# A place of their own for the weights of odd pairs, the first pair's sums on VectorE, the gelu's stores on SP's queue

## The chip, the cores and the metric

The kernel runs on one core of a Trainium2 chip. The metric is the device time of one execution, in microseconds (us); lower is better. The core has TensorE (PE, matrix multiply; PEld is its weight load), VectorE (DVE), ScalarE (ACT), GpSimd (POOL) and SyncE (SP). SP, ACT and POOL each have a queue on which transfers (DMAs) are issued; a queue works off its instructions in order, so an instruction that waits holds up all behind it.

## The reference

One decoder layer on 1024 tokens of width 1024, in float32:

```python
proj = x @ w_in                                   # one wide input projection, split into nine parts
y_a = rglru_branch(lru_x, lru_gate, ...)          # recurrent branch: h * gelu(lru_gate)
y_b = banded_window_attention(qb, kb, vb, 128, sinks)
y_c = dilated_attention(qc, kc, vc)               # three window/dilation patterns, combined
branch = einsum('bsnc,ncd->bsnd', stack([y_a, y_b, y_c]), w_branch)
merged = sum(sigmoid(gates) * branch, axis=2)     # gates: 3 x 1024 columns of proj
x = layer_norm(ALPHA * x + merged @ w_out)
h1, h3 = split(x @ w_ffn_in)                      # 2 x 2816 columns
x = layer_norm(ALPHA * x + (silu(h1) * h3) @ w_ffn_out)
```

What the change touches is the part of `x @ w_in` that makes the gates and the gelu gate, and `x @ w_ffn_in`.

## The kernel before

Every float32 matrix is split in two parts, a rounded one (hi, made by ScalarE with a copy to a 32-bit format that TensorE takes fast) and the rest (lo, made by VectorE with a subtraction). A product of 128x128 weights with 512 columns takes three matmuls: hi by hi, hi by lo, lo by hi.

The work runs in stages. First come the input projections, the recurrent branch and the two attentions (up to about 935 us). Then the **gate stage**: 12 pairs of gate columns and 3 pairs of gelu columns. Then the branch projections (`w_branch`), the output projection (`w_out`) with the first layer norm, the **FFN pairs** (22 of them), and `w_ffn_out` with the second layer norm.

A *pair* is two blocks of 128 weight columns, c = 0 and 1. The class `Pairs` (lines 832 to 987) computes both for all 1024 tokens with seven products in place of eight (a Strassen form of the 2x2 block product), each of 12 matmuls. The products are named by the operand of x: a00, s2, s1, s3, a01, s4, a11. For weights they need the blocks of the pair themselves (b0, b11) and four sums: t1, t2, t3 and t4. In a *fronted* pair a00 and a01 have been done in a stage before and their result is kept, so it has five products (60 matmuls); other pairs have seven (84). All 12 gate pairs and the first 4 FFN pairs are fronted; the gelu pairs (numbers 3, 6 and 9 of the gate stage's 15) and the other 18 FFN pairs aren't.

For each pair the weights go through this chain:
- `load` (line 878): two transfers of 512 KB on SP's queue, into two tiles with the tag w_raw. The pool `stage` has two such tiles in all, and both stages use it.
- `p1` (line 909): t1 and then t2 on POOL, each 128x512 (`wsum`, line 885). The tag t has two tiles.
- `wsplit` (line 890) of t2, then of t1: a copy on ScalarE into a tile ph, a subtraction on VectorE into a tile pl. There are 5 tiles of each in the gate stage (`n_p` = 5) and 7 in the FFN.
- `p5` (line 917): t3 on POOL, and its split. `p6` (line 921): t4 on POOL, written over t2 once that is split, then the split of b11 straight from the raw tile, then that of t4.
- `p2`, for a pair that isn't fronted: the split of the whole first raw tile, for a00 and a01.

`run` (line 971) strings them together. While pair j is computed, the steps for pair j+1 are issued at the seven points `between(i)` in front of j's products: `load` of j+1 at i = 1, `p1` and `p2` at 3, the split of t2 at 5, that of t1 and `p5` at 6, and `p6` of j+1 at its own i = 0. `p6` is the last to read the two raw tiles, so `load` of the next pair can't begin before it.

A product's result is added on VectorE (lines 946 to 968). A gate pair's four results are stored to sg_dram on ACT's queue. A gelu pair's four results go through `lg_finish` (line 692), two ScalarE and three VectorE instructions each, and its store to y_dram is issued on POOL's queue (line 699).

The operands s2, s3, s4 and part of the others are made by `x_sums` and `x_split` (lines 801, 1024) from four quarters of x; the last of these, number 3, lies in a tile of the pool `yx` (tag v, line 1032), and VectorE works on it when pair 0 begins. Later the same tile takes a quarter of the operand y for the branch stage (`load_y`, line 1060, called at pair 11). The transfers of `load_y` are issued on ACT's queue and carry an order-only dependence (line 1074) on the last copy of a weight that `wsplit` made.

The order of the instructions on each engine isn't written by hand alone: the program is given to a planner, which orders each engine's instructions by priority and by times that it simulates (`schedule_with_timeline_sim=True`). The chip then runs each engine in that order.

Of the kernel before, what the change touches and what calls it, by code (L numbers as in the profile page):

```python
# [9 lines left out]
F32 = mybir.dt.float32  # L10
# [33 lines left out]
class WeightStream:  # L44
# [41 lines left out]
    def _split(self):  # L86
        c = self.n_split
        self._dma(c + 2)
        raw = self.raw.pop(c)
        if self.dests[c] is None:  # L90
            hi = self.pool.tile([P, 1024], F32R, tag="w_hi", name="w_hi")
            lo = self.pool.tile([P, 1024], F32R, tag="w_lo", name="w_lo")
            self.ring.append(c)
        else:
            hi, lo = self.dests[c]()
        self.nc.scalar.copy(hi, raw)  # L96
        self.lo_engine.tensor_sub(lo, raw, hi.bitcast(F32))  # L97
        self.parts[c] = (hi, lo)
        self.n_split += 1
        self._dma(c + 3)  # L100
# [48 lines left out]
def trunk_kernel(ctx: ExitStack, tc: tile.TileContext, x, x_t, w_in, conv_w, conv_b, w_rg, b_rg, w_ig, b_ig,  # L149
# [542 lines left out]
    def lg_finish(ct, hf, z, u, hh):  # L692

        act.activation(u, z, AF.Square, scale=math.sqrt(0.044715))
        dve.scalar_tensor_tensor(u, u, 1.0, z, op0=OP.add, op1=OP.mult)
        act.activation(u, u, AF.Tanh, scale=math.sqrt(2.0 / math.pi))
        dve.scalar_tensor_tensor(u, u, 1.0, z, op0=OP.add, op1=OP.mult)
        dve.scalar_tensor_tensor(u, u, 0.5, hh, op0=OP.mult, op1=OP.mult)
        pool.dma_start(y_dram[0][ct, :, hf * HALF:(hf + 1) * HALF], u)
# [4 lines left out]
    def lg_evac(ct):  # L704
        def f(hf, acc):
            u, hh = [att4.tile([P, HALF], F32, tag=n, bufs=1, name=n) for n in ("gelu", "hh")]
            load_h(ct, hf, hh)
            lg_finish(ct, hf, acc, u, hh)
        return f
# [120 lines left out]
    recent = []  # L830

    class Pairs:
# [3 lines left out]
        def __init__(self, cols, ops, ring, p1pool, fronted, na, c00, c01, c10, c11, n_e=6, n_p=7):  # L836
            self.fronted = fronted
            self.cols, self.ops, self.ring, self.p1pool, self.na = cols, ops, ring, p1pool, na
            self.c00, self.c01, self.c10, self.c11 = c00, c01, c10, c11
            self.n_e, self.n_p = n_e, n_p  # L840
            self.raws, self.parts, self.front = {}, {}, {}
# [36 lines left out]
        def load(self, j):  # L878
            self.raws[j] = []
            for c in self.cols(j):  # L880
                t = stage.tile([P, 1024], F32, tag="w_raw", name="w_raw")
# [3 lines left out]
        def wsum(self, j, n, a, b, op):  # L885
            t = self.ring[0].tile([P, HALF], F32, tag="t", bufs=2, name="t")
            pool.tensor_tensor(t, a, b, op=op)  # L887
            self.raws[j, n] = t

        def wsplit(self, j, n, src, width=HALF):  # L890
            if width == HALF:
                hi = self.ring[0].tile([P, HALF], F32R, tag="ph", bufs=self.n_p, name="ph")
                lo = self.ring[0].tile([P, HALF], F32R, tag="pl", bufs=self.n_p, name="pl")
# [3 lines left out]
            recent[:] = [act.copy(hi, src)]  # L897
# [73 lines left out]
        def run(self, n, at=lambda j, i: None, first=None, done=0):  # L971

            first = first or self.prep(0)
            for f in first[done:6]:
                f()
            for j in range(n):
# [3 lines left out]
                def between(i):  # L980
                    if i == 0:
                        cur[6]()
                    elif nxt:
                        for f in {1: nxt[:1], 3: nxt[1:3], 5: nxt[3:4], 6: nxt[4:6]}.get(i, ()):
                            f()
                    at(j, i)
# [21 lines left out]
    def pair_out(j, c, hf, src):  # L1008
# [7 lines left out]
        else:  # L1016
            u, hh = [t[:, 2 * hf + c, :] for t in lgt]
            lg_finish(kinds[j] + c, hf, src, u, hh)

    gate = Pairs(pair_cols, xops, [gring], [gring], lambda j: j in gid, NG,  # L1020
                 lambda j, bank: pair_out(j, 0, 0, bank), lambda j, g: pair_out(j, 1, 0, g),
                 lambda j, g: pair_out(j, 0, 1, g), lambda j, v: pair_out(j, 1, 1, v), 4, 5)
# [37 lines left out]
    def load_y(n, hf):  # L1060
# [11 lines left out]
        for k in range(KT):  # L1072
            d = act.dma_start(yl[k].bitcast(F32), y_dram[n][k, :, hf * HALF:(hf + 1) * HALF])
            tc.add_manual_dep(d.ins, recent[-1].ins.name, NO_SYNC, reason="not earlier than the pairs' weights")
# [322 lines left out]
    ffn = Pairs(lambda j: [w_cols(w_ffn_in, c) for c in (j * P, FF + j * P)], ops, sringp, [frp], lambda j: j < NA, NA,  # L1397
# [152 lines left out]
```

## Time and profile before

| | us |
|---|---|
| median of 3 runs | 2243.51 (2243.04 to 2245.42) |
| the profiled execution, its own time | 2241.2 |
| its span, first to last instruction | 2239.4 |
| TensorE busy | 2170.8 (97%) |
| VectorE busy | 1424.7 (64%) |
| ScalarE busy | 969.7 (43%) |
| POOL busy | 559.5 (25%) |
| mean granted TensorE clock | 0.992 of full speed |

"Busy" is the time in which an engine had an instruction under way; matmuls are pipelined, so a new one begins each 0.23 us though each lasts 0.39 us. In a row of the timeline, what stands in square brackets is the idle time of the engine in front of that instruction and what ended it. The rows themselves stand in a section below.

### The profile page before, as it was taken

How to read it: one execution, taken by the hardware profiler on the slowest of the kernel's cores; microseconds unless marked ns; L12 is line 12 of the kernel's file. 1: busy time of each engine (PE TensorE's matmuls, PEld its weight loads, DVE VectorE, ACT ScalarE, POOL GpSimd, SP SyncE). 2: the span in 40 equal slices, each digit the busy share in tenths (PEclk: the TensorE clock that was granted, in tenths of full speed). 3: DMA queues.
4: the chain of work that ended last, by engine and by line, in shares of the span. 5: the costliest groups of instructions: out<-in, count | busy, mean ns of one | idle time of the engine just before them, and what ended most of it. 6: DMA issues, size and time to landing. Idle time of an engine off the chain costs nothing. (4 is left out here: it accounts for less than half of the span.)

```text
span 2239.4 us, 29667 instructions
## 1 busy us (share of the span) xinstructions
PE 2170.8 (97%) x10981; PEld 1834.5 (82%) x10981; DVE 1424.7 (64%) x2695; ACT 969.7 (43%) x1826; POOL 559.5 (25%) x506
## 2 busy tenths in 40 slices
PE   8999999999999999899999999999999999999998
PEld 6787888988889888677777888888788888888786
DVE  7888888876777776655565334459565444453735
ACT  4765766665655656522324223223333333332321
POOL 2332222212222234233341000002344444300301
PEclk9999999999999999999999999999999999999999
DMA  5123123122222144444457334244232222254543
GB/s 151 48 80 97 48 65 81 49 48 64 48 56 56 30 105 139 130 137 137 141 174 253 131 106 132 94 146 154 87 104 85 85 85 85 85 193 148 183 157 119
DMA packets 228401, 241.57 MB, mean 108 GB/s; under 512 B 11489, under 2 KB 170273, under 8 KB 228257
## 3 DMA queue, kind: packets, MB, share of 16 engines
q1 hardware_dynamic: 184864, 135.28, 19.9%
q0 software_dynamic: 18336, 57.73, 8.8%
q10 hardware_dynamic: 25056, 46.67, 6.1%
q8 instruction: 86, 1.41, 0.3%
q14 instruction: 59, 0.48, 0.1%
HBM read 177.51 MB, written 51.64 MB: 102 GB/s over the span
## 5 line engine op out<-in xcount | busy, mean ns | idle before, releaser
L187 PE MATMUL acc<-xh,w_hi 128*128 128x512 f32 x688 | 274.6, 399 | 13.0 <-ACT w_hi L96 6.9
L187 PE MATMUL acc<-xl,w_hi 128*128 128x512 f32 x688 | 272.1, 395 | 0.0
L187 PE MATMUL acc<-xh,w_lo 128*128 128x512 f32 x688 | 271.6, 395 | 0.0
L96 ACT CAST w_hi<-w_raw 128x1024 fp32r<-128x1024 f32 x130 | 136.7, 1052 | 242.9 <-PE acc L187 192.5
L897 ACT CAST ph<-t 128x512 fp32r<-128x512 f32 x148 | 89.7, 620 | 309.6 <-POOL t L887 219.7
L887 POOL TENSOR_TENSOR t<-w_raw 128x512 f32<-128x512 f32 x74 | 109.0, 1472 | 313.8 <-DMA w_raw<-in_w_ffn_in_dram 193.8
L97 DVE TENSOR_TENSOR w_lo<-w_raw,w_hi 128x1024 fp32r<-128x1024 f32 x89 | 113.8, 1279 | 112.2 <-ACT w_hi L96 111.9
L898 DVE TENSOR_TENSOR pl<-t,ph 128x512 fp32r<-128x512 f32 x148 | 111.3, 759 | 113.0 <-ACT ph L897 112.9
L187 PEld LDWEIGHTS acc<-xh,w_hi 128*128 128x128 f32 x688 | 130.4, 189 | 38.8 <-ACT w_hi L96 6.9
L539 POOL DMA_DIRECT2D y_dram<-yp x96 | 51.6, 537 | 428.4 <-DVE yp L538 341.0
L549 DVE TENSOR_TENSOR pt_l<-pt,pt_h 128x512 fp32r<-128x512 f32 (+3 forms) x256 | 144.2, 572 | 21.3 <-ACT pt_h L548 19.0
L548 ACT CAST pt_h<-pt 128x512 fp32r<-128x512 f32 (+3 forms) x256 | 124.4, 501 | 70.1 <-PE pt L544 65.5
L187 PEld LDWEIGHTS acc<-xh,w_lo 128*128 128x128 f32 x688 | 130.1, 189 | 25.5 <-DVE w_lo L97 0.8
L187 PEld LDWEIGHTS acc<-xl,w_hi 128*128 128x128 f32 x688 | 130.4, 190 | 23.5
L544 PE MATMUL pt<-ident,p 128*128 128x128 f32 x816 | 128.0, 276 | 4.3 <-DVE pt_l L549 3.5
L97 POOL TENSOR_TENSOR w_lo<-w_raw,w_hi 128x1024 fp32r<-128x1024 f32 x41 | 98.9, 2412 | 113.0 <-ACT w_hi L96 106.9
L187 PE MATMUL o<-pt_h,v 128*128 128x256 f32 (+1 forms) x464 | 117.0, 274 | 2.0 <-DVE yp L538 1.5
L187 PE MATMUL acc<-w_lo,gh 128*128 128x512 f32 x288 | 113.5, 394 | 4.1 <-DVE w_lo L97 4.0
L631 ACT ACTIVATE p<-p,small 128x128 f32<-128x128 f32 (+7 forms) x128 | 99.7, 779 | 34.9 <-DVE small L628 33.8
L187 PE MATMUL o<-pt_l,v 128*128 128x256 f32 (+1 forms) x464 | 113.1, 284 | 1.3 <-DVE pt_l L549 1.3
L187 PE MATMUL acc<-w_hi,gl 128*128 128x512 f32 x288 | 112.8, 392 | 0.0
L187 PE MATMUL s<-kh,q 128*128 128x256 f32 (+3 forms) x320 | 104.4, 335 | 1.7 <-DVE small L628 1.0
(303 smaller groups left out, 5927.6 us busy)
## 6 DMA issues: line engine op xcount, KB each, us to landing
w_raw<-in_w_in_dram SPq DMA_DIRECT2D x88, 512.0 KB, 3.9
w_raw<-in_w_ffn_in_dram SPq DMA_DIRECT2D x48, 512.0 KB, 3.8
w_raw<-in_w_ffn_out_dram SPq DMA_DIRECT2D x47, 512.0 KB, 3.7
w_raw<-in_w_branch_dram SPq DMA_DIRECT2D x24, 512.0 KB, 4.9
sg<-sg_dram POOLq DMA_DIRECT2D x24, 512.0 KB, 3.9
g_dram<-e POOLq DMA_DIRECT2D x44, 256.0 KB, 3.2
sg_dram<-e ACTq DMA_DIRECT2D x39, 256.0 KB, 2.6
yl<-y_dram ACTq DMA_DIRECT2D x32, 256.0 KB, 6.0
```

What stands on the lines that cost most here:

```text
L96: self.nc.scalar.copy(hi, raw)
L97: self.lo_engine.tensor_sub(lo, raw, hi.bitcast(F32))
L187: pe.matmul(o, a, b, start=start, stop=stop, skip_group_check=True)
L539: pool.dma_start(dst, yp[:, :n])
L544: pe.transpose(pt[:, i * P:(i + 1) * P], b, ident)
L548: act.copy(dst_h, v)
L549: dve.tensor_sub(dst_l, v, dst_h.bitcast(F32))
L631: act.activation(p[:, :n], p[:, :n], AF.Exp, bias=m, scale=-1.0, accum_out=sm[:, 1:2])
L887: pool.tensor_tensor(t, a, b, op=op)
L897: recent[:] = [act.copy(hi, src)]
L898: dve.tensor_sub(lo, src, hi.bitcast(F32))
```

## The change

1. **Place.** `load` no longer takes its tiles from the tag w_raw alone but from a function `room`. Even pairs use w_raw as before. Odd pairs of the gate stage use the tile v of `yx` (pairs 1 to 9) and then the two tiles with the tag w_hi (pairs 11 and 13). Odd pairs of the FFN use two tiles of their own in the FFN's ring; in exchange the ring has 5 tiles ph and pl of each where it had 7.
2. **Order of issue.** `load(1)` is issued ahead of the first pair, and `load(j+2)` at `between(1)` of pair j. `p1` of j+1 moves from point 3 to 1, `p2` and the split of t2 to 2, the split of t1 to 3, `p5` to 4.
3. **First sums.** t1, t2 and t3 of pair 0 of the gate stage are computed on VectorE, not on POOL. (t4 stays on POOL.)
4. **Stores.** The four stores of a gelu pair are issued on SP's queue, the one that also loads the weights, not on POOL's.
5. **Order of y.** The order-only dependence of `load_y` is now on the last weight copy of any kind, also on those of the stream `W` that feeds the branch stage.

```diff
 class WeightStream:
-        self.nc.scalar.copy(hi, raw)
+        self.recent = self.nc.scalar.copy(hi, raw)
 ...
-    def lg_finish(ct, hf, z, u, hh):
+    def lg_finish(ct, hf, z, u, hh, queue):
-        pool.dma_start(y_dram[0][ct, :, hf * HALF:(hf + 1) * HALF], u)
+        queue.dma_start(y_dram[0][ct, :, hf * HALF:(hf + 1) * HALF], u)
 ...
         def load(self, j):
             self.raws[j] = []
-            for c in self.cols(j):
-                t = stage.tile([P, 1024], F32, tag="w_raw", name="w_raw")
+            for i, c in enumerate(self.cols(j)):
+                t = self.room(j, i)
                 sync.dma_start(t.rearrange("p (a b) -> p a b", b=P), c)
 ...
         def wsum(self, j, n, a, b, op):
-            pool.tensor_tensor(t, a, b, op=op)
+            (dve if self is gate and j == 0 else pool).tensor_tensor(t, a, b, op=op)
 ...
-                hi = self.ring[0].tile([P, HALF], F32R, tag="ph", bufs=self.n_p, name="ph")
-                lo = self.ring[0].tile([P, HALF], F32R, tag="pl", bufs=self.n_p, name="pl")
+                hi = self.ring[0].tile([P, HALF], F32R, tag="ph", bufs=5, name="ph")
+                lo = self.ring[0].tile([P, HALF], F32R, tag="pl", bufs=5, name="pl")
 ...
-            recent[:] = [act.copy(hi, src)]
+            W.recent = act.copy(hi, src)
 ...
+            self.load(1)
             for j in range(n):
 ...
-                        for f in {1: nxt[:1], 3: nxt[1:3], 5: nxt[3:4], 6: nxt[4:6]}.get(i, ()):
+                        for f in {1: nxt[1:2], 2: nxt[2:4], 3: nxt[4:5], 4: nxt[5:6]}.get(i, ()):
                             f()
+                        if i == 1 and j + 2 < n:
+                            self.load(j + 2)
 ...
+    def gate_room(j, i):
+        if j % 2 == 0:
+            return raw_tile()
+        if j > NP - 2:
+            return raw_tile("w_hi")
+        if not spare:
+            spare.append(yx.tile([P, 4, HALF], F32, tag="v", name="w_raw"))
+        return spare[0].rearrange("p a b -> p (a b)")[:, i * D:(i + 1) * D]
 ...
-            tc.add_manual_dep(d.ins, recent[-1].ins.name, NO_SYNC, reason="not earlier than the pairs' weights")
+            tc.add_manual_dep(d.ins, W.recent.ins.name, NO_SYNC, reason="not earlier than the pairs' weights")
 ...
     ffn = Pairs(...,
+                lambda j, i: raw_tile() if j % 2 == 0 else sringp[0].tile([P, 1024], F32, tag="w_raw", bufs=2, name="w_raw"),
```

## Rows read from the trace of the kernel before

**Rows 1.** Busy time by stretch. Columns: stretch and its length in us; busy us and number of instructions of PE, PEld, DVE, ACT, POOL; granted TensorE clock; share of the DMA engines; GB/s. The gate stage, and the part of the FFN pairs that aren't fronted.

```profile
945.00:1185.00 240.00, 223.97 (x945) 181.64 (x944) 137.19 (x201) 70.21 (x120) 90.06 (x72) 0.96 0.46 145
1650.00:1935.00 285.00, 284.83 (x1257) 235.59 (x1256) 142.39 (x201) 89.83 (x139) 119.16 (x93) 1.00 0.27 86
```

**Rows 2.** Who PE waited for, 930 to 1220 us: us in total, times, longest. Then the same for 1570 to 2010 us.

```profile
PE acc L187 <- ACT ph L897: 15.8, 6, 4.7
...
PE acc L187 <- ACT ph L897: 4.2, 3, 1.6
```

**Rows 3.** PE's timeline in the gate stage: start, us, what, and the idle time in front. First the first and the last of 48 matmuls without a gap, then the five instructions in front of which PE had waited more than 1 us for a weight.

```profile
965.81 0.39 PE L187 MATMUL acc<-gs2h,ph 128*128 128x512 f32 x1
976.46 0.39 PE L187 MATMUL acc<-gs4h,pl 128*128 128x512 f32 x1
...
949.90 0.50 PE L187 MATMUL acc<-gs2h,ph 128*128 128x512 f32 x1 [3.19 <-ACT ph L897]
978.10 0.50 PE L187 MATMUL acc<-gs2h,ph 128*128 128x512 f32 x1 [1.25 <-ACT ph L897]
1026.87 0.80 PE L187 MATMUL acc<-gs2h,ph 128*128 128x512 f32 x1 [4.71 <-ACT ph L897]
1079.15 0.50 PE L187 MATMUL acc<-gs2h,ph 128*128 128x512 f32 x1 [2.98 <-ACT ph L897]
1130.40 0.50 PE L187 MATMUL acc<-gs2h,ph 128*128 128x512 f32 x1 [3.02 <-ACT ph L897]
```

**Rows 4.** Busy time by stretch (columns as in rows 1): the four stretches of 20 us in the gate stage in which the granted clock is below 1.00, and the one in which the branch stage begins.

```profile
945.00:965.00 20.00, 16.61 (x65) 12.80 (x64) 12.60 (x17) 6.59 (x13) 10.04 (x6) 0.91 0.36 113
1025.00:1045.00 20.00, 18.13 (x68) 14.77 (x69) 9.80 (x14) 5.09 (x8) 7.48 (x8) 0.83 0.40 132
1065.00:1085.00 20.00, 17.02 (x68) 13.45 (x67) 13.97 (x22) 7.04 (x12) 7.22 (x8) 0.91 0.51 169
1125.00:1145.00 20.00, 16.98 (x68) 13.43 (x67) 10.58 (x16) 4.04 (x7) 9.98 (x8) 0.91 0.56 174
1205.00:1225.00 20.00, 18.88 (x83) 14.98 (x82) 14.27 (x21) 14.78 (x22) 1.06 (x2) 1.00 0.77 271
```

**Rows 5.** Who the queue of SP waited for, and who POOL waited for, 945 to 1185 us.

```profile
SPq L882 <- POOL t L923: 136.3, 14, 12.3
...
POOL y_dram L699 <- DVE u L698: 20.7, 6, 4.9
```

**Rows 6.** The chain of work that ended last, where it passes through the weights of one gate pair: start, us, what.

```profile
1156.21 3.67 DMA w_raw<-in_w_in_dram
1160.05 1.30 POOL t L887
1161.42 1.30 POOL t L887
1162.74 0.63 ACT ph L897
1163.39 0.70 DVE pl L898
1164.16 1.68 POOL t L923
...
1169.14 3.90 DMA w_raw<-in_w_in_dram
```

**Rows 7.** Timelines of POOL, DVE and SP's queue around pair 0: t1 of pair 0 on POOL; the first and the last of 8 VectorE instructions that ran back to back beside it; the last VectorE instruction that works on the quarters of x (the eleventh after those eight); the loads of pair 1 (two issues, 5.68 us from the first to the end of the second).

```profile
941.74 6.12 POOL L887 TENSOR_TENSOR t<-w_raw 128x512 f32<-128x512 f32 x1 [10.54 <-DMA w_raw<-in_w_in_dram]
...
941.84 0.68 DVE L1029 TENSOR_TENSOR gs3l<-xq,gs3h 128x512 fp32r<-128x512 f32 x1
...
946.05 0.68 DVE L1029 TENSOR_TENSOR xl<-xq,xh 128x512 fp32r<-128x512 f32 x1
...
958.10 0.68 DVE L1029 TENSOR_TENSOR gs4l<-xq,gs4h 128x512 fp32r<-128x512 f32 x1
...
952.34 5.68 SPq L882 DMA_DIRECT2D w_raw<-in_w_in_dram  x2
```

**Rows 8.** Timelines of DVE and POOL in the pairs that follow a gelu pair: the subtraction that frees the tile of t4 in each of the three (pairs 4, 7 and 10), then, for the third, t1 of pair 11 on POOL.

```profile
1019.17 0.68 DVE L898 TENSOR_TENSOR pl<-t,ph 128x512 fp32r<-128x512 f32 x1
...
1071.49 0.68 DVE L898 TENSOR_TENSOR pl<-t,ph 128x512 fp32r<-128x512 f32 x1
...
1123.20 0.69 DVE L898 TENSOR_TENSOR pl<-t,ph 128x512 fp32r<-128x512 f32 x1
...
1126.38 1.65 POOL L887 TENSOR_TENSOR t<-w_raw 128x512 f32<-128x512 f32 x1 [3.44 <-DVE e L946]
```

**Rows 9.** PE's timeline in the FFN: the two instructions in front of which it waited longest for a weight of a fronted pair after pair 0 (pairs 2 and 3).

```profile
1608.46 0.50 PE L187 MATMUL acc<-s2h,ph 128*128 128x512 f32 x1 [1.48 <-ACT ph L897]
1623.49 0.50 PE L187 MATMUL acc<-s2h,ph 128*128 128x512 f32 x1 [1.06 <-ACT ph L897]
```

**Rows 10.** ACT's timeline: a copy into a tile ph, in the gate stage, that waited for a product. Then ACT's queue and engine where the branch stage begins: the first transfers of the second half of y, and the copy of the second branch weight; and the first matmul that uses that half's lo part.

```profile
1102.54 0.62 ACT L897 CAST ph<-t 128x512 fp32r<-128x512 f32 x1 [1.74 <-PE acc L187]
...
1183.00 0.81 ACTq L1073 DMA_DIRECT2D yl<-y_dram  x2
1186.03 1.06 ACT L96 CAST w_hi<-w_raw 128x1024 fp32r<-128x1024 f32 x1 [1.54 <-DMA w_raw<-in_w_branch_dram]
...
1204.19 0.39 PE L187 MATMUL acc<-yl,w_hi 128*128 128x512 f32 x1
```

More of the change, by code (lines that the diff above doesn't have):

```diff
@@ L707, in f @@
             load_h(ct, hf, hh)
-            lg_finish(ct, hf, acc, u, hh)
+            lg_finish(ct, hf, acc, u, hh, pool)
         return f
@@ L826, in trunk_kernel, with __init__ @@
     acc8 = mk_pool(ctx, "acc8", bufs=8, space=PSUM)
-    recent = []
     class Pairs:
-        def __init__(self, cols, ops, ring, p1pool, fronted, na, c00, c01, c10, c11, n_e=6, n_p=7):
-            self.fronted = fronted
+        def __init__(self, cols, ops, ring, p1pool, room, fronted, na, c00, c01, c10, c11, n_e=6):
+            self.room, self.fronted = room, fronted
             self.cols, self.ops, self.ring, self.p1pool, self.na = cols, ops, ring, p1pool, na
             self.c00, self.c01, self.c10, self.c11 = c00, c01, c10, c11
-            self.n_e, self.n_p = n_e, n_p
+            self.n_e = n_e
             self.raws, self.parts, self.front = {}, {}, {}
@@ L1017, in pair_out, with raw_tile @@
             u, hh = [t[:, 2 * hf + c, :] for t in lgt]
-            lg_finish(kinds[j] + c, hf, src, u, hh)
-    gate = Pairs(pair_cols, xops, [gring], [gring], lambda j: j in gid, NG,
+            lg_finish(kinds[j] + c, hf, src, u, hh, sync)
+    def raw_tile(tag="w_raw", dtype=F32):
+        return stage.tile([P, 1024], dtype, tag=tag, name="w_raw")
+    def gate_room(j, i):
[6 more added lines that the diff above has]
+        return spare[0].rearrange("p a b -> p (a b)")[:, i * D:(i + 1) * D]
+    spare = []
+    gate = Pairs(pair_cols, xops, [gring], [gring], gate_room, lambda j: j in gid, NG,
                  lambda j, bank: pair_out(j, 0, 0, bank), lambda j, g: pair_out(j, 1, 0, g),
-                 lambda j, g: pair_out(j, 0, 1, g), lambda j, v: pair_out(j, 1, 1, v), 4, 5)
+                 lambda j, g: pair_out(j, 0, 1, g), lambda j, v: pair_out(j, 1, 1, v), 4)
     def x_split(k):
@@ L1395, in ffn_c10 @@
         pool.dma_start(g_dram[1, j], g)
-    ffn = Pairs(lambda j: [w_cols(w_ffn_in, c) for c in (j * P, FF + j * P)], ops, sringp, [frp], lambda j: j < NA, NA,
+    ffn = Pairs(lambda j: [w_cols(w_ffn_in, c) for c in (j * P, FF + j * P)], ops, sringp, [frp],
+                lambda j, i: raw_tile() if j % 2 == 0 else sringp[0].tile([P, 1024], F32, tag="w_raw", bufs=2, name="w_raw"),
+                lambda j: j < NA, NA,
                 ffn_c00, ffn_c01, ffn_c10, ffn_c11)
```

## The prediction

> **What bounds the kernel now.** I read the page first (TensorE is busy 97% of the span, so only what leaves it idle or slow can be won), then the stretches, then who TensorE waited for. In the stretches the reader sees two different places. In the gate stage TensorE is busy 224.0 of 240 us and its mean clock is 0.96; in the unfronted FFN pairs it is busy 284.8 of 285 us at full clock [rows 1]. So the gate stage can gain and the 18 unfronted FFN pairs can't. The waits name one cause: 15.8 us in the gate stage and 4.2 us in the FFN for ScalarE's copy of a weight into ph [rows 2].
>
> The timeline of TensorE shows the pace and the stalls. 48 matmuls without a gap take (976.46 - 965.81) / 47 = 0.2266 us each, so a fronted pair of 60 takes 13.6 us and one of 84 takes 19.0 us. The stalls are 3.19 us ahead of pair 0 and 4.71, 2.98 and 3.02 us in the pairs behind the three gelu pairs; two short ones make up most of the rest [rows 3]. The second cost stands in the clock: 0.91, 0.83, 0.91 and 0.91 of full speed in just the four stretches that hold the four long stalls [rows 4]. Half of the clock's time lost counts as (1 - clock) x 20 us: 1.8 + 3.4 + 1.8 + 1.8 = 8.8 us. Behind the 1.25 us stall no such stretch shows.
>
> Why the weights are late: SP's queue waited 136.3 us in all for t4 on POOL [rows 5], since the loads need the raw tiles that t4 reads last. The chain of waits shows the loop of one pair: load, t1, t2, copy, subtraction, t4, next load, from 1156.21 to 1169.14 = 12.9 us [rows 6]. TensorE needs 13.6 us for the pair, so the loop has 0.7 us to spare, and a gelu pair's work on ScalarE and VectorE, which pushes back the splits, uses up more than that.
>
> **The change part by part.** The sum is made against the profiled execution: 2241.2 us, which is its span of 2239.4 and 1.8 us around it. The median of the runs is 2.3 us above it.
>
> *Place and order of issue (1, 2).* The load leaves the loop of one pair. It may begin when the pair two before has done its t4, a whole pair (13.6 us) earlier than needed; from issue to the next sum takes 1160.05 - 1156.21 = 3.8 us [rows 6]. What is late next is the tag t with its two tiles: t1 of the next pair takes the tile of t4, which is free when t4's split ends. From t1 to the copy's end it is 1163.39 - 1160.05 = 3.3 us [rows 6]. In a plain pair t4's split may be written as soon as the previous pair's last product is over; with copy and subtraction (0.63 + 0.70) the next pair's first weight stands 4.7 us into a pair of 13.6 us. So the 1.25 us of pair 2 and the smaller waits go.
>
> Behind a gelu pair I take the times at which t4's split ended before: 1019.85, 1072.17 and 1123.89 [rows 8]. With 3.3 us on top the first weights would stand at 1023.2, 1075.5 and 1127.2. TensorE began to wait at 1026.87 - 4.71 = 1022.2, at 1076.2 and at 1127.4 [rows 3]. What is left is 1.0 + 0 + 0 = 1.0 us of the 10.7, too short for the clock to fall if 1.25 us was.
>
> *First sums (3).* t1 of pair 0 took 6.12 us on POOL from 941.74, as long as VectorE ran its instructions back to back beside it [rows 7]; the same instruction takes 1.30 us elsewhere [rows 6]. On VectorE two sums cost two places in its line, which moves on every (946.05 - 941.84) / 7 = 0.60 us [rows 7]. The weight could stand at about 941.8 + 1.2 + 0.6 = 943.6, and TensorE is ready at 949.90 - 3.19 = 946.7, so this stall goes. What is late next is pair 1: its place is the tile of the last quarter of x, and VectorE reads that until 958.68 before [rows 7]. From 941.84 it has 8 + 11 instructions up to there and now 3 sums: 22 x 0.60 = 13.2 us, that is 955.1 at the latest, and 14 x 0.60 later than 941.84, 950.2, if all work on x went first. From a load's issue to the copy's end it is 1163.39 - 1156.21 = 7.2 us [rows 6], if the two loads run beside each other, and 3.7 us more if one after the other. TensorE wants pair 1 at 946.7 + 13.6 = 960.3. So the new stall is between 0 (957.4) and 5.7 us (966.0); I take 955.1 + 7.2 - 960.3 = 2.0 us, because the DMA engines are only 0.36 busy in that stretch [rows 4].
>
> A rule of the Trainium skill bears on this (SBUF — State Buffer, section "SBUF: two separate sides"): VectorE and GpSimd share one pair of ports under an exclusive lock, which a VectorE instruction with two SBUF inputs and a GpSimd instruction keep from each other for a whole instruction. The 6.12 us agree with it, and show more: the loser waited through eight instructions, not one. By this rule POOL's other sums would suffer too where VectorE is dense; that is the first rival below, priced from rows.
>
> *Stores (4).* POOL waited 20.7 us in six places, up to 4.9 us, for the gelu's last VectorE instruction with a store in hand [rows 5]. Now SP waits there, with the loads of the pair after next behind it. They have 13.6 us of cover, so I cost it at 0; without the cover it would be up to 4.9 us for each gelu pair. On POOL the sums get free by as much, but t's tile comes later than that: 0 gained.
>
> *FFN.* The stalls of the fronted pairs behind pair 0, 1.48 + 1.06 = 2.5 us, have the same cause [rows 9] and go; the remaining 1.6 of the 4.2 us stand ahead of pair 0, whose first load isn't moved: 0. Two tiles ph and pl less: a copy may only be written when the product five splits back is over. ScalarE waited 1.74 us for that in the gate stage with five tiles [rows 10]; the weights now are made two to four products earlier. 0, with the third rival for the other end.
>
> *Order of y (5).* The second half of y was issued from 1183.00; now it comes behind the copy of the second branch weight, which ends at 1187.1: up to 4.1 us later. Its lo part is first used at 1204.19 [rows 10], so 0. Later parts of y now come behind weights, not before them; TensorE lost 1.1 us in that stretch [rows 4]. Between a gain of 1.1 and a loss of 2; I take 0.
>
> *Sum.* Gate stage 15.8 + 8.8 - 2.0 - 1.0 = 21.6; FFN 2.5; together 24.1 us. 2241.2 - 24.1 = 2217.1, and with the 2.3 us of the median 2219.4, so 2219.5 us.
>
> **Rivals.** *POOL's sums held up by a dense VectorE (chance 0.20).* With the load gone from the loop, t1 and t2 behind a gelu pair fall where VectorE works off the gelu. For: beside such work t1 took 1.65 us [rows 8]. Against: the gelu's instructions may spread out earlier, when subtractions no longer wait for late weights. If each of the two sums waits for one VectorE instruction (0.68) and takes 1.65, the weight stands 2 x 2.33 + 0.63 = 5.3 us after t4's split, at 1025.1, 1077.5 and 1129.2: stalls of 3.0 + 1.3 + 1.8 = 6.1, that is 5.1 more than in my sum, and the half clock's 3.4 us stays at the first. 2219.5 + 8.5 = 2228.
>
> *The wait only changes its name (0.10).* Behind the gelu pairs VectorE's own line is what is late, and pair 1 waits for the quarter of x as long as pair 0 did. Then the three stalls and their clock stay, 10.7 + 7.0 - 1.0 = 16.7 us, and pair 1 loses 5.7 + 1.8 - 2.0 = 5.5: 2219.5 + 22.2 = 2242, no change. For: TensorE's stall and VectorE's burst lie together in time. Against: SP's long waits for t4 [rows 5] put the loads in front of it.
>
> *Slower: the FFN's ring (0.08).* With five tiles in place of seven ScalarE, which works in order, may stand in front of a copy whose tile is still read and hold the results' copies behind it, in each of the 18 unfronted pairs. At 1.48 us per pair, the nearest stall of an FFN pair [rows 9], 26.6 us are lost: with the gate's 21.6 gained and the 2.5 us of the fronted pairs not, the time is 2243.5 - 21.6 + 26.6 = 2248.5. It decides from 21.6 / 18 = 1.2 us per pair. Against it: five products lie between a tile's last use and its next need.
>
> **How the numbers follow.** The forecast has 0.58, with its own range of 2214 (nothing left of the 15.8, 8.8 and 4.2 us, and 1.1 more: 29.9 gained) to 2225 (pair 1 at 5.7). 0.04 are for still less than that lower end, by an order of the planner that closes other gaps. The range for 8 in 10 must take in the first rival and the work it prices: 2212 to 2236. A measurement of this kernel can tell 0.2%, 4.5 us, from no change. Faster by more than that: 0.58 + 0.20 + 0.04 = 0.82; the same 0.10; slower 0.08.
>
> **What would show it.** After the change SP's waits for t4 should no longer end in a wait of TensorE: in the gate stage the waits for line 897's copy fall from 15.8 to about 3 us, and the clock stays at 1.00 in all stretches but perhaps the first. t1 of pair 0 on VectorE lasts about 0.7 us. If the first rival holds, POOL's sums behind pairs 3, 6 and 9 last well over 1.3 us, and TensorE still waits there. If the third holds, TensorE is below 100% between the FFN's pair 4 and its end. The prediction is wrong if the gate stage, from pair 0 to the first branch product, isn't about 22 us shorter, or if another stage takes back more than 3 us.

## The result, and the profile after

The changed kernel takes 2224.74 us (median of 4 runs, 2221.16 to 2227.84) where the kernel before took 2243.69 us in the same session (2243.04 to 2245.42). The ratio is 0.9914 with a 95% interval of 0.9893 to 0.9935: 19.0 us faster. The forecast was 2219.5 with a range of 2212 to 2236.

The stages, cut where TensorE's timeline shows the first or last matmul of each, in us. "Ready" is the start of the first matmul less its idle time. The last column is a second profile of the same changed kernel.

| stage | before | after | after, second profile |
|---|---|---|---|
| to TensorE ready for the gate pairs | 946.71 | 950.45 | 949.53 |
| gate pairs | 249.54 | 230.94 | 229.69 |
| branch stage | 259.81 | 258.91 | 259.57 |
| to TensorE ready for the FFN pairs | 124.14 | 124.63 | 123.15 |
| FFN pairs | 402.80 | 399.74 | 399.75 |
| second FFN product | 247.41 | 249.17 | 247.91 |
| last matmul to end of span | 8.99 | 11.86 | 11.90 |
| span | 2239.4 | 2225.7 | 2221.5 |

The busy times by stretch of the changed kernel, columns as in [rows 1]; the first two answer to those rows, the others to [rows 4]:

```profile
945.00:1185.00 240.00, 234.13 (x1022) 191.98 (x1021) 152.86 (x222) 78.04 (x131) 85.00 (x58) 0.99 0.52 166
1650.00:1935.00 285.00, 285.00 (x1259) 235.97 (x1259) 134.46 (x195) 87.53 (x135) 100.38 (x90) 1.00 0.26 84
...
945.00:965.00 20.00, 17.57 (x76) 13.36 (x75) 17.39 (x28) 7.53 (x14) 4.08 (x1) 1.00 0.56 176
965.00:985.00 20.00, 16.56 (x66) 12.96 (x65) 10.88 (x15) 6.06 (x10) 11.34 (x8) 0.91 0.45 139
...
1025.00:1045.00 20.00, 20.00 (x90) 16.58 (x89) 11.41 (x17) 4.25 (x7) 9.44 (x7) 1.00 0.61 194
1065.00:1085.00 20.00, 20.00 (x90) 16.58 (x89) 16.54 (x26) 7.26 (x12) 9.05 (x6) 1.00 0.70 223
1125.00:1145.00 20.00, 20.00 (x90) 16.57 (x89) 15.68 (x22) 7.78 (x15) 7.62 (x5) 1.00 0.75 247
1205.00:1225.00 20.00, 20.00 (x90) 16.57 (x89) 10.69 (x17) 10.52 (x17) 0.53 (x1) 1.00 0.85 277
```

In the same 240 us TensorE does 1022 matmuls in place of 945. The three stretches behind the gelu pairs, whose clock was 0.83, 0.91 and 0.91, are full at 1.00. What is left of idle time and of half clock lies in the first 40 us.

Who TensorE waited for, 940 to 1185 us and then 1500 to 2000 us (answers to [rows 2]), and SP's queue, 945 to 1185 us (answers to [rows 5]): us in total, times, longest.

```profile
PE acc L187 <- ACT ph L896: 4.6, 2, 2.6
PE acc L187 <- DVE e L950: 0.8, 1, 0.8
PE acc L187 <- DVE pl L897: 0.5, 1, 0.5
...
PE acc L187 <- ACT ph L896: 1.6, 1, 1.6
...
SPq L880 <- POOL t L922: 75.7, 10, 16.4
SPq L699 <- DVE u L698: 38.1, 9, 9.8
```

The wait for ph falls from 15.8 to 4.6 us and, in the FFN, from 4.2 to 1.6 us. SP's queue still waits 75.7 us for POOL's t4 and now 38.1 us for the gelu, and behind the gelu pairs TensorE waits for neither. TensorE's timeline shows where the rest is (start, us, idle time in front; answers to [rows 3]): pair 0 twice, pair 1, and one wait for VectorE's e.

```profile
952.38 0.50 PE L187 MATMUL acc<-gs2h,ph 128*128 128x512 f32 x1 [1.93 <-ACT ph L896]
954.14 0.50 PE L187 MATMUL acc<-gs2h,pl 128*128 128x512 f32 x1 [0.51 <-DVE pl L897]
969.84 0.79 PE L187 MATMUL acc<-gs2h,ph 128*128 128x512 f32 x1 [2.65 <-ACT ph L896]
980.44 0.47 PE L187 MATMUL acc<-gs4h,ph 128*128 128x512 f32 x1 [0.79 <-DVE e L950]
```

Why pair 0 and pair 1 are late is read from the timelines of the other engines, 947 to 970 us (answers to [rows 7]).

```profile
947.39 0.68 DVE L886 TENSOR_TENSOR t<-w_raw 128x512 f32<-128x512 f32 x1
...
951.00 0.68 DVE L886 TENSOR_TENSOR t<-w_raw,t 128x512 f32<-128x512 f32 x1
...
956.42 0.68 DVE L1044 TENSOR_TENSOR gs4l<-xq,gs4h 128x512 fp32r<-128x512 f32 x1
957.18 1.62 DVE L897 TENSOR_TENSOR pl<-t,ph 128x512 fp32r<-128x512 f32 x1
...
951.71 1.14 ACT L896 CAST ph<-t 128x512 fp32r<-128x512 f32 x2 [1.78 <-DVE t L886]
...
954.17 4.08 POOL L922 TENSOR_TENSOR t<-w_raw,t 128x512 f32<-128x512 f32 x1 [19.22 <-DVE pl L897]
966.52 1.27 POOL L886 TENSOR_TENSOR t<-w_raw 128x512 f32<-128x512 f32 x1 [8.27 <-DMA w_raw<-in_w_in_dram]
...
958.28 2.08 SPq L880 DMA_DIRECT2D w_raw<-in_w_in_dram  x3
...
969.17 0.62 ACT L896 CAST ph<-t 128x512 fp32r<-128x512 f32 x1 [10.26 <-POOL t L886]
```

Pair 0: the sums t1 and t2 on VectorE take 0.68 us each, but they stand 3.6 us apart (947.39 and 951.00), with five instructions of work on x between them, so the copy ends its first tile only at about 952.3. Pair 1: its place is free when the last VectorE read of that quarter of x ends, at 956.42 + 0.68 = 957.10. But SP's queue stands until POOL's t4 of pair 0 ends (954.17 + 4.08 = 958.25): a load of pair 2, which must wait for that t4, is ahead of pair 1's loads in SP's order. It goes out at 958.28 and pair 1's two behind it, the first at 958.95. t1 of pair 1 begins 8.2 us after 958.28 and the copy ends at 969.79.

### The profile page after: what moved, and what is told of

It is laid out like the page before. It is cut to its first block, busy times and chain, and to the rows that moved or that the text cites. A ratio compares the mean times of both kernels' runs of the same rounds, so it can differ in the third digit from the quotient of the medians.

```text
span 2225.7 us, 29666 instructions
## 1 busy us (share of the span) xinstructions
PE 2167.7 (97%) x10981; PEld 1835.3 (82%) x10981; DVE 1425.1 (64%) x2698; ACT 972.4 (44%) x1826; POOL 534.3 (24%) x491
## 4 chain that ended last, share of the span: by engine, by line
PE 80%; DVE 9%; issue 4%; DMA 3%; ACT 2%; POOL 1%; ACTq 0%; DVEq 0%; SPq 0%; POOLq 0%
PE acc L187 69%; PE o L187 4%; PE s L187 4%; PE pt L544 4%; DVE xc L387 1%; DVE w_lo L97 1%; DMA xin<-in_x_t_dram 1%; DMA w_raw<-in_w_in_dram 1%; DVE r L1304 1%; DVE r L1283 1%; DVE r L1301 0%; DVE xc L384 0%; DVE pt_l L549 0%; DVE m L426 0%; DVE stats L1293 0%
## 5 line engine op out<-in xcount | busy, mean ns | idle before, releaser
L886 POOL TENSOR_TENSOR t<-w_raw 128x512 f32<-128x512 f32 x72 | 97.1, 1348 | 133.7 <-DVE pl L897 96.8
L897 DVE TENSOR_TENSOR pl<-t,ph 128x512 fp32r<-128x512 f32 x148 | 106.3, 724 | 32.4 <-ACT ph L896 32.2
```

The lines of the kernel that those rows point to most:

```text
L886: (dve if self is gate and j == 0 else pool).tensor_tensor(t, a, b, op=op)
L897: dve.tensor_sub(lo, src, hi.bitcast(F32))
```

## The experiments

The results of all runs, with the stages that decide. Time is the median; the ratio is to the kernel before on the same chip (2244.45, 2244.94 and 2244.51 us in the three sessions).

| run | time | ratio, 95% | gate pairs | FFN pairs | last matmul to end |
|---|---|---|---|---|---|
| changed kernel again | 2224.8 | 0.9914 (0.9899 to 0.9930) | 229.69 | 399.75 | 11.90 |
| one place, new order | 2245.25 | 1.0000 (0.9991 to 1.0010) | 249.26 | 405.19 | 11.89 |
| new places, old order | 2223.8 | 0.9911 (0.9894 to 0.9929) | 230.26 | 399.76 | 11.92 |
| first sums back on POOL | 2229.77 | 0.9932 (0.9912 to 0.9951) | 234.80 | 400.63 | 11.88 |
| pair 1 in w_hi | 2218.03 | 0.9886 (0.9868 to 0.9904) | 226.76 | 399.74 | 11.90 |
| stores back on POOL | 2217.59 | 0.9882 (0.9860 to 0.9903) | 229.21 | 399.71 | 9.01 |
| the same, again | 2219.08 | 0.9884 (0.9867 to 0.9901) | 229.25 | 399.76 | 9.02 |
| before, stores on SP | 2244.92 | 1.0000 (0.9991 to 1.0008) | 249.89 | 403.45 | 11.89 |
| FFN ring of four | 2222.6 | 0.9900 (0.9884 to 0.9915) | 229.97 | 400.80 | 11.92 |
| order of y undone | 2232.62 | 0.9942 (0.9924 to 0.9960) | 233.76 | 399.75 | 11.85 |
| pair 1 in w_hi, stores on ACT | 2220.27 | 0.9893 (0.9873 to 0.9913) | 226.53 | 399.76 | 11.91 |
| pair 1 in w_hi, stores on POOL | 2214.87 | 0.9867 (0.9849 to 0.9884) | 226.53 | 399.74 | 9.01 |

**The changed kernel again.** No edit.

> The changed kernel once more, unaltered, for its spread and a second trace. The times fell in two groups before (2221.2 and 2221.7, 2227.8 and 2227.8 us). Theory A (granted clock in stages the change doesn't touch): the gate stage, from the moment TensorE is ready for pair 0 to the last product of the 15 pairs, takes 230.9 us again within 1 us, and what differs between executions stands in stages before 930 us or after 1940 us. Theory B (the change itself has two outcomes, for instance at pair 1): the gate stage differs by 3 to 6 us between the groups.

The median repeats to 0.1 us, and the six times lie between 2223.4 and 2228.1, without two groups. The gate stage comes out 1.25 us shorter than in the first profile, which meets neither theory, and the residual stalls are the same ones (1.91, 0.50 and 2.53 us). The 4.2 us between the two spans are spread over several stages. The stage ahead of it, whose code no kernel here changes, lasted between 946.71 and 951.02 us over all profiles of this case. So a single profile tells a stage to about 2 us, and the total only to a few.

**Place or order.** First the new order of issue with one place for all pairs:

```diff
-        if j % 2 == 0:
+        if True:
             return raw_tile()
 ...
-                lambda j, i: raw_tile() if j % 2 == 0 else sringp[0].tile([P, 1024], F32, tag="w_raw", bufs=2, name="w_raw"),
+                lambda j, i: raw_tile(),
```

> The counterpart: the new order of issue with the one place of the kernel before for all pairs (both stages), everything else as changed. My theory: the load still waits for t4 of the pair in front, so the order alone gives nothing: stalls behind the three gelu pairs of 2 to 5 us each, granted clock under 0.95 in the stretches that hold them, gate stage 240 to 250 us (249.54 before), time 2234 to 2245. Rival, that order is what counts: gate stage within 3 us of the changed kernel's 230.9, time under 2228.

All of the gain is gone: 2245.25 us, the time of before. TensorE's timeline of this kernel shows the old stalls back behind the gelu pairs and one at 1177 (start, us, idle time in front):

```profile
1027.76 0.62 PE L187 MATMUL acc<-gs2h,ph 128*128 128x512 f32 x1 [2.80 <-ACT ph L896]
1078.62 0.50 PE L187 MATMUL acc<-gs2h,ph 128*128 128x512 f32 x1 [2.73 <-ACT ph L896]
1129.54 0.50 PE L187 MATMUL acc<-gs2h,ph 128*128 128x512 f32 x1 [2.71 <-ACT ph L896]
1177.01 0.50 PE L187 MATMUL acc<-gs2h,ph 128*128 128x512 f32 x1 [2.00 <-ACT ph L896]
```

Its busy times from 985 to 1185 us (columns as in [rows 1]) give 188.27 busy and a clock of 0.96:

```profile
985.00:1185.00 200.00, 188.27 (x789) 152.69 (x788) 116.58 (x168) 58.80 (x99) 66.32 (x48) 0.96 0.47 148
```

Then the counterpart, the new places with the old order of issue:

```diff
-            self.load(1)
 ...
-                        for f in {1: nxt[1:2], 2: nxt[2:4], 3: nxt[4:5], 4: nxt[5:6]}.get(i, ()):
+                        for f in {1: nxt[:1], 3: nxt[1:3], 5: nxt[3:4], 6: nxt[4:6]}.get(i, ()):
                             f()
-                        if i == 1 and j + 2 < n:
-                            self.load(j + 2)
```

> The changed kernel with its new places for odd pairs, but with the order of issue of the kernel before: splits of the next pair behind products 1, 3, 3, 5, 6, 6, and no load ahead of the pair's products (both stages). My theory: what stalled the gate stage was the load that could not begin before t4; a place of its own takes it out of the loop even if its line in the program is later. Then the stalls behind the three gelu pairs stay away (TensorE 100% busy from 985 us on, at most 1 us in all) and the gate stage lasts 230 to 234 us (230.94 and 229.69 in the two profiles of the changed kernel, 249.54 before), the time 2225 to 2229. Rival, that the earlier order of issue did it: the stalls behind gelu pairs come back with 2 to 4 us each and the half clock with them, gate stage 240 to 250, time 2234 to 2244.

2223.8 us, and the same stretch of this kernel is full, as expected:

```profile
985.00:1185.00 200.00, 200.00 (x884) 165.62 (x883) 126.09 (x183) 65.36 (x108) 68.47 (x50) 1.00 0.52 165
```

The two kernels have the other parts of the change in common, so of these two parts the places take the stalls away and the order takes none. No run has the places without all the rest, but the runs below that undo one other part each keep the stalls behind the gelu pairs away too. The chain of [rows 6] is the reason: as long as the load's tile is the one that t4 reads, it starts behind t4, however early it stands in the program. With one place SP's queue still waits for t4 14 times, as before, 111.1 us in all; with the new places it waits 10 times, 75.7 us.

**First sums.** Back on POOL:

```diff
-            (dve if self is gate and j == 0 else pool).tensor_tensor(t, a, b, op=op)
+            pool.tensor_tensor(t, a, b, op=op)
```

> Only the third edit undone: t1, t2 and t3 of pair 0 on POOL again. My theory (VectorE is dense with the work on x there, and POOL's sum waits beside it): t1 of pair 0 takes about 6 us on POOL, TensorE waits about 3 us ahead of pair 0 in place of 1.9 + 0.5, pair 1 stays about as it is; the total is 0 to 3 us above the changed kernel. Rival (the first sums carry the gain): the total rises by 10 us or more. Second rival (three sums on a dense VectorE delay the work on x and with it pair 1): the total falls by 1 to 4 us, because pair 1's stall of 2.65 us and its low clock go.

Undoing it costs 5.0 us (2229.77 against 2224.8), more than the 0 to 3 expected, and 3.9 to 5.1 us of the gate stage. The timelines of TensorE, POOL and VectorE in this kernel:

```profile
952.97 0.50 PE L187 MATMUL acc<-gs2h,ph 128*128 128x512 f32 x1 [3.17 <-ACT ph L896]
972.87 0.80 PE L187 MATMUL acc<-gs2h,ph 128*128 128x512 f32 x1 [3.86 <-ACT ph L896]
...
944.77 6.15 POOL L886 TENSOR_TENSOR t<-w_raw 128x512 f32<-128x512 f32 x1 [11.94 <-DMA w_raw<-in_w_in_dram]
...
953.71 1.66 POOL L922 TENSOR_TENSOR t<-w_raw,t 128x512 f32<-128x512 f32 x1 [1.45 <-DVE pl L897]
...
952.95 0.69 DVE L897 TENSOR_TENSOR pl<-t,ph 128x512 fp32r<-128x512 f32 x1 [3.14 <-ACT ph L896]
...
961.15 0.68 DVE L1044 TENSOR_TENSOR gs4l<-xq,gs4h 128x512 fp32r<-128x512 f32 x1
```

t1 on POOL takes 6.15 us, as before (6.12, [rows 7]), and pair 1 is later too. That isn't by t4, which ends at 953.71 + 1.66 = 955.37 here, 2.9 us sooner than in the changed kernel. It is by pair 1's place: VectorE stands for 3.14 us at a subtraction that waits for the copy of the late sum, so its last read of that quarter of x ends at 961.83 in place of 957.10, and pair 1's loads go out at 961.90. So this part is worth more than the stall it was aimed at, though that stall only shrinks from 3.2 to 2.4 us.

**Where pair 1 lands.** Its loads go to the two w_hi tiles, which are free at the start of the gate stage:

```diff
-        if j > NP - 2:
+        if j == 1 or j > NP - 2:
             return raw_tile("w_hi")
```

> Pair 1's two raw tiles are taken from the two w_hi tiles, which are free early, in place of the tile that holds the last quarter of x. My theory (pair 1 waits because SP's queue stands in front of POOL's t4 of pair 0, which takes 4.1 us beside a dense VectorE, and because VectorE reads that quarter until 957): pair 1's loads are issued before 947 us, the stall of 2.65 us ahead of pair 1 and the low clock behind it (1.8 us) go, the total falls by 3 to 5 us. Rival (pair 1 is late because POOL's sums wait for VectorE, wherever the weights lie): the loads are early but POOL's t1 of pair 1 isn't, and the total stays within 1 us.

The stall of pair 1 is gone and the gate stage is 2.9 to 4.2 us shorter, with the half clock of 965 to 985 us gone as well; the time is 2218.0, 6.8 us less than the changed kernel's 2224.8 where 3 to 5 were expected. The reading of the timelines above, that pair 1 was late by its place and by its turn on SP's queue, holds; the run doesn't part the two.

**The stores' queue.** Back on POOL's queue in the changed kernel:

```diff
-            lg_finish(kinds[j] + c, hf, src, u, hh, sync)
+            lg_finish(kinds[j] + c, hf, src, u, hh, pool)
```

> Only the fourth edit undone: the gelu pairs' stores on POOL's queue again. My theory (the tile of t4 frees later than POOL does): TensorE doesn't wait behind the gelu pairs, total within 2 us of the changed kernel. Rival (the stores held POOL up, and freeing it made the gain): waits of about 3 us come back behind pairs 3, 6 and 9, with the low clock, and the total rises by 10 to 17 us.

A miss for both theories: nothing stalls behind the gelu pairs, as the first has it, so the stores never held POOL's sums up where it counts, but the kernel is 7.2 us faster. A second run was made to see whether it repeats:

> The changed kernel with the gelu's stores on POOL's queue a second time, to part its 7 us into what is the kernel's and what is the execution's. If only the tail is the kernel's: 2224.3 (mean of the changed kernel's two medians) - 2.9 = 2221.4 or so, tail 9.0, gate stage 229 to 231. If all of it is the kernel's: 2217 to 2218 again.

It does: 2219.1, or 5.7 us under the changed kernel. Two things show in both profiles. The gate stage is 0.4 to 1.7 us shorter; pair 1 waits 0.85 and 0.99 us in place of 2.65 and 2.53. But that lies ahead of the first gelu store, with the same order on VectorE and SP, and the half clock has only moved ahead of pair 1 (0.91 from 945 to 965 us in both), so that TensorE itself comes later; it isn't shown to be the queue's doing. And the end of the span comes 9.0 us after the last matmul, not 11.9. The last issue on SP's queue ends and the span ends, in the changed kernel, at 2219.31 + 0.94 = 2220.25 and 2225.7; with the stores on POOL at 2211.81 and 2214.4. First the row of the one, then of the other:

```profile
2219.31 0.94 SPq L1504 DMA_DIRECT2D out_dram<-r  x2
```

```profile
2210.87 0.94 SPq L1504 DMA_DIRECT2D out_dram<-r  x2
```

What stands in those last us is in the list of line 1562, the end of the program (number of instructions, shortest, median and longest in ns, start of the first and the last): POOL closes its program with an instruction DRAIN of 12.87 us, which begins beside POOL's last sum, at 2212.04, and ends at 2224.91. With the stores on POOL it takes 3.97 us and ends at 2207.60, ahead of SP's last issue. First the row of the changed kernel, then the other:

```profile
L1562 POOLq DRAIN  x3: 51/98/12868, 2212.0 to 2225.4; - x3
```

```profile
L1562 POOLq DRAIN  x3: 51/93/3967, 2203.6 to 2214.1; - x3
```

Two more runs ask about the queue. The stores alone, in the kernel before:

```diff
-        pool.dma_start(y_dram[0][ct, :, hf * HALF:(hf + 1) * HALF], u)
+        (sync if W.n_gate else pool).dma_start(y_dram[0][ct, :, hf * HALF:(hf + 1) * HALF], u)
```

> The kernel before with one part of the change alone: the gelu's stores of the gate stage on SP's queue. The last stage of the table, from TensorE's last matmul to the end of the span, was 9.0 us in the three profiles with those stores on POOL's queue and 11.9 in the seven with them on SP's. Theory tail (the stores' queue sets it): here 11.9 us instead of 8.99, everything else as before within 2 us, time 2244.5 + 2.9 = 2247.4. Rival (the tail goes by execution, or by another part of the change): tail 9.0, time 2244 to 2245. In the gate stage the loads of this kernel wait for t4 on SP's queue, and a store in front of them adds a wait for VectorE: if that matters there, the gate stage is 250 to 254 us in place of 249.54.

The end of the profile is 11.89 us long, as the first theory says, but the time doesn't follow: 2244.92 against 2244.51, and the interval ends at 1.0008, 1.8 us. And the third queue, in the version with pair 1 in w_hi:

```diff
-            lg_finish(kinds[j] + c, hf, src, u, hh, sync)
+            lg_finish(kinds[j] + c, hf, src, u, hh, act)
```

> The version with pair 1 in w_hi and the gelu's stores on ScalarE's queue: neither SP's nor POOL's. It asks what lengthens the end. If a store on SP's queue does it, the tail is 9.0 us here as with POOL; if it takes POOL's queue to have the stores for a short tail, it is 11.9. In the gate stage ScalarE, which works in order, now stands at each store until VectorE's last gelu instruction: if the copies behind it have cover, the gate stage is 226 to 228 us and the time 2214 to 2218; if not, stalls of up to 4.9 us (the longest that POOL waited so) behind each gelu pair, gate stage 230 to 240, time 2219 to 2232.

11.91 us again, and the gate stage at 226.53: ScalarE's standing at the stores is covered. The time, 2220.27, is above the 2214 to 2218 expected, and why is open. Over all profiles the end is 9.0 us in the four with these stores on POOL's queue and 11.85 to 11.92 in the ten others. The same holds of the DRAIN: 3.97 us in the four, whose POOL queue issues 260 transfers, and 12.87 us in the ten, where it issues 248. So what the end of the span waits for is the DRAIN; why it is longer after fewer transfers is not shown. Since the kernel before doesn't pay them in its time, they aren't proven to be the cause. What is shown is that the choice of SP costs the changed kernel about 6 us; 2.9 of them stand at the end of the span, and the rest is not located. With pair 1 in w_hi the same choice costs 3.2 us (2218.03 against 2214.87, below).

**The FFN's ring.** Four tiles ph and pl in place of five:

```diff
-                hi = self.ring[0].tile([P, HALF], F32R, tag="ph", bufs=5, name="ph")
+                hi = self.ring[0].tile([P, HALF], F32R, tag="ph", bufs=5 if self is gate else 4, name="ph")
```

(and the same for pl)

> The changed kernel with four tiles ph and pl in the FFN in place of five (the gate keeps five). It asks how near the ring of five is to costing anything. If five tiles have slack (my theory), four cost little: FFN pairs 399.74 us in the changed kernel, here 399.5 to 403, time 2224 to 2228. Rival (the prediction's third): the ring is what the FFN's copies wait for, so each of the 18 unfronted pairs loses 0.5 to 1.5 us: FFN pairs 409 to 427 us, time 2233 to 2252; then five would have been at its limit as well.

400.80 us against 399.74, and the time is that of the changed kernel. Even four tiles cost no more than 1.1 us over the whole FFN, so five have slack.

**The order of y.** The loads of y wait for the gate's own last copy again:

```diff
-            W.recent = act.copy(hi, src)
+            W.recent = self.recent = act.copy(hi, src)
 ...
-            tc.add_manual_dep(d.ins, W.recent.ins.name, NO_SYNC, reason="not earlier than the pairs' weights")
+            tc.add_manual_dep(d.ins, gate.recent.ins.name, NO_SYNC, reason="not earlier than the pairs' weights")
```

> The changed kernel with the order of y as before: the loads of y wait for the gate's own last copy, not for the last copy of any weight. The prediction put 0 on this part (-1.1 to +2). If 0 is right: gate pairs plus branch stage 489.3 to 490.5 us (489.85 and 489.26 in the two profiles of the changed kernel, 509.35 before), time 2222.5 to 2226. Rival, that the part is worth 1 us or more, as the 0.9 us between 259.81 and 258.91 could mean: the two stages together 490.8 to 492, and TensorE's short waits for yl and w_lo come back near the first branch products.

Outside both ranges: 2232.62 us, 7.8 us slower, and the two stages take 233.76 + 261.86 = 495.6 us, 5.8 more than in the changed kernel's first profile. TensorE's timeline of this kernel has two stalls where the branch stage begins, and the busy times by stretch (columns as in [rows 1]) a clock of 0.93 behind the second:

```profile
1181.63 0.47 PE L187 MATMUL acc<-xh,ph 128*128 128x512 f32 x1 [2.12 <-DVE e L954]
1204.20 1.01 PE L187 MATMUL acc<-yv,w_hi 128*128 128x512 f32 x2 [1.89 <-ACT w_hi L96]
```

```profile
1205.00:1225.00 20.00, 20.00 (x83) 16.08 (x82) 9.46 (x13) 8.74 (x12) 1.21 (x3) 0.93 0.53 158
```

VectorE and ScalarE are what TensorE waits for, and their timelines say with what they were busy: four subtractions for y stand ahead of the sum e, and y's copies ahead of the branch weight:

```profile
1178.39 2.49 DVE L1086 TENSOR_TENSOR yl<-yl,yh 128x512 fp32r<-128x512 f32 x4
1180.80 0.68 DVE L954 TENSOR_TENSOR e<-e,acc 128x512 f32<-128x512 f32 x1
...
1202.08 1.12 ACT L1085 CAST yh<-yl 128x512 fp32r<-128x512 f32 x2
1203.11 1.04 ACT L96 CAST w_hi<-w_raw 128x1024 fp32r<-128x1024 f32 x1
```

The gate's last copy begins at 1165.91 in this kernel where it began at 1183.87 in the kernel before, and what hangs on it alone moves ahead with it: y's first loads go out at 1165.04, ahead of the second branch weight's copy (1176.16, after 9.6 us of waiting for its transfer; 1172.40 in the changed kernel). So this part earns little against the kernel before, but without it the change would give back 8 of its us.

**The two better versions together.** Pair 1 in w_hi, stores on POOL's queue:

```diff
-        if j > NP - 2:
+        if j == 1 or j > NP - 2:
 ...
-            lg_finish(kinds[j] + c, hf, src, u, hh, sync)
+            lg_finish(kinds[j] + c, hf, src, u, hh, pool)
```

> Both versions that came out below the changed kernel put together: pair 1's weights land in the two w_hi tiles, and the gelu's stores go back to POOL's queue. If their gains add (6.7 and 7.2 us against the changed kernel on the same chip): 2224.8 - 13.9 = 2210.9. By the stage table they overlap: both profiles show a shorter way to the gate stage (948.3 and 948.0 against 949.5) and that part counts once, and the tail of 9.0 in place of 11.9 us belongs to the stores' version alone: gate stage 226 to 227, tail 9.0, time 2213 to 2217. If the stores' gain was only an execution's luck: 2218 as with w_hi alone.

2214.87 us, within the range for overlapping gains: 30.1 us under the kernel before on its chip (2244.94), 9.9 under the changed one, and the fastest measured. From 965 us to the end of the gate stage its stretches are full; what is left is 1.80 us ahead of pair 0 and the clock behind it.

## Why the prediction was right, and where it was off

The time lies within the forecast's own range (2214 to 2225), at its very top, and the mechanism was the right one: the load left the loop of one pair, and the two runs on place and order show that it was this and not the order of issue. The terms, predicted and then measured in the two profiles of the changed kernel, as us gained:

| term | predicted | measured |
|---|---|---|
| gate pairs | 21.6 | 18.6 and 19.9 |
| branch stage | 0 | 0.9 and 0.2 |
| FFN pairs | 2.5 | 3.1 and 3.1 |
| all other stages | 0 | -8.9 and -5.2 |

- *Place and order.* The stalls behind the gelu pairs were to keep 1.0 us; they kept none, and their clock came back whole. The sum took t4's split at its old time plus 3.3 us, and that split itself moved forward (behind the first gelu pair from 1019.85 to 1014.69). Of the order of issue the prediction claimed no price of its own, and it has none.
- *First sums, the stall of pair 0.* Mis-sized. It was to vanish, with the weight at 943.6, 3.1 us before TensorE is ready. t1 ran at 947.39 and t2 at 951.00, so the copy's first tile stood 1.8 us after TensorE was ready (at 950.45 in this profile), and 1.93 + 0.51 us of stall stayed. The prediction gave the two sums the first two places in VectorE's line. The planner spread them among the work on x.
- *First sums, the stall of pair 1.* Predicted 2.0 us (0 to 5.7), measured 2.65 plus 0.79 for e and (1 - 0.91) x 20 = 1.8 us of half clock, 5.2 in all. That the stall itself came so near is luck: errors cancel. Counted from the moment TensorE is ready, 946.7 in the prediction and 950.45 here, x was read until 6.7 us, sooner than the 8.4 predicted. But pair 1's first load went out at 8.5 us (958.95). The step that was missing is SP's queue: the prediction named what is late next on VectorE, but not that a load of pair 2 stands in front and waits for POOL's t4, to 958.25. From the load's issue to the copy's end it took 10.8 us; the prediction chose 7.2 for loads side by side and had 10.9 as the other end. And TensorE, itself held up at pair 0, came for the weight at 16.7 us, not 13.6. (Its reading that VectorE read that quarter until 958.68 before should be 958.10 + 0.68 = 958.78; nothing rests on it.)
- *Stores.* Costed at 0; putting them back is worth 5.7 to 7.2 us in the changed kernel. The cover the prediction named did hold (no stall behind a gelu pair, with 38.1 us of waiting on SP's queue). The cost lies elsewhere: 2.9 us of the span are at the end of the program, where the prediction didn't look, and the rest is not located.
- *FFN.* 2.5 predicted, 3.1 measured; the stalls of pairs 2 and 3 [rows 9] are gone and pair 0's stays at 1.61 us, as said.
- *Order of y.* The 0 against the kernel before is right (0.2 to 0.9). The reason wasn't: it was worked out with the old times of the copies, as if nothing else had moved, and without this part the new times cost 7.8 us.
- *All other stages.* 3.7 of the 8.9 us are the stage ahead of the gate. No part of the change is aimed at it, and before's own 946.71 was the shortest of all; the kernel before with only its stores moved shows 949.56. There is one profile of the kernel before, so what of this is the kernel's is open. By these 3.7 us the prediction's last sign of being wrong, another stage that takes back more than 3 us, did show in the first profile (2.8 us in the second). The sum was made against a profiled execution 2.5 us under its own session's median, and the profile after was 3.0 us over its. By the medians the change gained 19.0 us, not the 13.7 that the two spans show.

Of the rivals, *the wait only changes its name* fell with the full stretches from 985 us on; its half on pair 1 struck in part (2.65 us of its 5.7, and the 1.8 of half clock). *The FFN's ring* fell with the ring of four. *POOL's sums held up by a dense VectorE* is half true: behind the first two gelu pairs t2 takes 2.21 us on POOL, where [rows 6] has 1.30, and the other sums there last 1.28 to 1.68. But the weights now have time enough, and TensorE doesn't wait there. Where VectorE is densest the rival did strike, in a place it hadn't named: t4 of pair 0, 4.08 us, in front of pair 1's loads.

POOL's timeline of the changed kernel, the first sum behind the first gelu pair that is drawn out:

```profile
1021.95 2.21 POOL L886 TENSOR_TENSOR t<-w_raw,t 128x512 f32<-128x512 f32 x1 [5.49 <-DVE pl L897]
```

## What to carry to other kernels

Where a load waited for the last reader of its tile, an earlier line in the program did nothing here and a second tile took the stalls away, so look for a tile that is idle at that time before tuning the order. When weights come earlier, what is tied to "the last copy" by an order-only dependence comes earlier too; leaving it so cost 7.8 us here. And a sum against one profile should take the stages that the change doesn't touch from more than one execution.

## What the runs showed of the hardware

POOL's sum beside VectorE was not slowed by a share. It was kept out, and then it kept VectorE out. In the rows above, POOL's t4 begins at 954.17 while VectorE's instructions follow each other without a gap until 957.10. t4 ends at 958.25, 1.15 us behind the gap, which is about what such a sum takes alone (1.26 to 1.30). VectorE's next instruction begins at 957.18 and takes 1.62 us in place of 0.68: it is the one that waits now. The Trainium skill (SBUF — State Buffer, section "SBUF: two separate sides") calls the port pair of the two engines an exclusive lock, held for a whole instruction; both numbers agree with it.

Whether POOL waits for a gap differs from place to place. Here it did, over the whole burst. In the rows below, from the timelines of VectorE and POOL in the same changed kernel, t4 of a later pair gets in between two VectorE instructions that follow each other without a gap, and the second of them takes 1.78 us. What decides between the two isn't shown.

```profile
1132.88 0.68 DVE L1086 TENSOR_TENSOR yv<-yv 128x512 fp32r<-128x512 f32 x1
1133.48 1.78 DVE L897 TENSOR_TENSOR pl<-t,ph 128x512 fp32r<-128x512 f32 x1
...
1133.04 1.68 POOL L922 TENSOR_TENSOR t<-w_raw,t 128x512 f32<-128x512 f32 x1 [4.56 <-DVE pl L897]
```

The clock fell behind the stall of 2.65 us at 969.84 (0.91 in 965 to 985 us), and stayed at 1.00 in the 20 us with the stalls of 1.93 and 0.51 us. It fell as well in kernels whose stall ahead of pair 0 was shorter: 0.91 from 945 to 965 us with 1.90 us, with the stores back on POOL, and with 1.80 us in the fastest version. So in these rows the length of one stall does not tell by itself whether the clock falls.
